# Attention's two ends in a two-layer transformer kernel: the order of the query scale, the number of leading weight units, and the place of the last weight casts

## The chip, the cores and the metric

The kernel runs on one core of a Trainium2 chip. The metric is the device time of one execution in microseconds; before the change the median of three runs is 1749.79 us (1749.52 to 1751.82). The core has five engines that run side by side, each through its own queue in order: TensorE (PE, matrix products into PSUM), VectorE (DVE), ScalarE (ACT), GpSimd (POOL) and SyncE (SP, which here only issues DMAs). PEld in the profile is TensorE's loading of the stationary operand, which overlaps its products.

## The reference

Two layers work on 256 tokens of width 2048. The first is a Fourier mixer; the second, which the change touches, is attention over a window with 256 further context keys, and a final norm:

```python
q, k, v, z = split(h @ w_in)                  # 64 query heads, 8 key/value heads, 64 wide
q = axial_rope(q, rows, cols); k = axial_rope(k, rows, cols)
s = q @ concat(k_window, k_context).T * 64 ** -0.5
p = softmax(concat(s + mask, sink))[..., :-1]
y = (p @ concat(v_window, v_context)) * silu(z)
x = x + gate * (y @ w_out[1])
out = rmsnorm(x, final_g)
```

All inputs are float32. By their shapes, query weights, gate weights and output weights of the attention layer are 33.5 MB each; the page counts 419 MB read from memory in all.

## The kernel before, in words

Products are made to nearly float32 precision from two parts of each operand: a high part (a cast, on ScalarE) and a low part (what is left, a subtraction, on VectorE or GpSimd). `mm3` (lines 144 to 147) then issues three matmuls: high by high, high by low, low by high. A weight load of 1 MB (`raw`, line 47, three buffers, SP's queue) is split in halves by `half_split` (which records lines 66 and 67) or, for half-precision parts with a power-of-two scale, by `split16` (lines 137 and 138). The parts lie in a pool of six buffers (`ws`), so parts of three halves fit when each half needs two.

The order on each engine is not the program's order. A planner sorts the instructions of each engine when the program is built, by program order as priority, by its own estimate of when operands and buffers are ready, and by edges written by hand: `with tc.issue_after(x)` makes the instructions of the block that run on x's engine come behind x.

The attention stage has three sorts of work.

*Filler units* (`units`, `emit_unit`) are the weight products, 142 of them in a fixed order: eight units for each of eight query head groups ("q"), two for each of 32 gate blocks ("z"), and 14 for the first quarter of the output projection ("o"). A q or an o unit is 12 matmuls over 512 columns, a z unit 24 over 256. When a unit is emitted, the weights of the next one are prepared (`prep`). Emission of the last unit of a q group calls `finish_q`; that of the second z unit ends a gate block.

*Query finishing.* `finish_q` takes the two halves (128 tokens each) of a head group's queries from PSUM: ScalarE squares them for a sum (line 1365), VectorE turns them by the rotary step (`roped`, lines 1129 to 1138: one product with the cosines, two with the sines, one sum), and four short VectorE instructions (lines 1371 to 1374) make a power-of-two scale `up` and its counterpart `sc`. `q_parts` (lines 1382 and 1383) makes the scaled high and low parts of each half and turns them: by DMA for seven head groups, and for head group 0 by TensorE (`pe_turn`, line 1392, eight transposes of 128 by 128 and a copy from PSUM, line 1393, on ScalarE for the first half and on VectorE for the second). The calls of `q_parts` are kept in `defer` and made some units later.

*Blocks.* 32 blocks of two heads each. `stage_s(b)` makes the scores (12 matmuls, line 1500), the mask and maximum (VectorE, line 1503), the exponentials (ScalarE, line 1507), the normed parts of the probabilities (ScalarE, line 1522, and VectorE, line 1523), and turns them: by DMA for blocks 0 to 30, and for block 31 by `pe_turn`, called from the block loop. `stage_o(b)` multiplies the turned probabilities with the values (24 matmuls, line 1534).

The order around the change is this: `first` = 10 units, then the query parts of head group 0 and their transposes, and then for b = 0 to 32: `stage_s(b)`, four filler units, `stage_o(b - 1)`. In the last round (b = 32) there are no scores; three units run, then the 32 transposes for block 31, `stage_o(31)`, and one unit. TensorE is held to this order by `issue_after(pe_last[0])`, where `pe_last` is the last matmul so far; the transposes of `pe_turn` do not set it.

Behind it comes the output projection's next half (`wo1b`): 16 groups of 1 MB, each split (lines 137 and 138) and multiplied in 24 matmuls. The splits of every group are held behind `f_last`, the last parts of block 31's probabilities. `first_rest` puts the last two units of the first quarter between groups 1 and 2.

Of the kernel before, what the change touches and what calls it, by code (L numbers as in the profile page):

```python
# [17 lines left out]
P = 128  # L18
# [14 lines left out]
def tile_dit(ctx: ExitStack, tc: tile.TileContext, a: dict, out: bass.AP):  # L33
    nc = tc.nc
    V, S, PE, GP = nc.vector, nc.scalar, nc.tensor, nc.gpsimd
# [4 lines left out]
    actp = ctx.enter_context(tc.tile_pool(name="act", bufs=33))  # L40
# [14 lines left out]
    def act(dt=F32):  # L55
        return actp.tile([P, 512], dt, tag="act", name="act")
# [582 lines left out]
    for g in range(G):  # L639
        for j in {13: (8, 9), 14: (10, 11)}.get(g, (g - 5,) if 5 <= g < 13 else ()):  # L640
            t = up.tile([P, 1024], F32, name="pz", tag="pz", bufs=1)
# [217 lines left out]
    with tc.tile_pool(name="yp", reuse_waits="tile", bufs=32) as ypool:  # L859
# [39 lines left out]
        if True:  # L899
# [44 lines left out]
            for b in range(4, NB):  # L944
# [9 lines left out]
                o = psum()  # L954
# [76 lines left out]
        for i in range(32):  # L1031
            sw, kg = i // 16, i % 16
            if kg == 0:
                o = [psum() for _ in range(8)]
# [23 lines left out]
            if kg >= 12:  # L1058
                for k in range(sw * 8 + (kg - 12) * 2, sw * 8 + (kg - 12) * 2 + 2):
                    t = act()  # L1060
# [43 lines left out]
    with tc.issue_after(st_end[0]):  # L1104
        o = psum()
# [23 lines left out]
    def roped(dst, src, tb, pool, tag="rt", eng=V, tab=rope):  # L1129
        t2 = pool.tile([P, 512], F32, tag=tag, name="rt")  # L1130
        sv = src.rearrange("p (h d) -> p h d", d=64)
        eng.tensor_tensor(dst.rearrange("p (h d) -> p h d", d=64), sv, tab[:, 0, tb, :].unsqueeze(1).broadcast_to([P, 8, 64]), op=ALU.mult)
        s4 = src.rearrange("p (h a t i) -> p h a t i", a=2, t=2, i=16)
        t4 = t2.rearrange("p (h a t i) -> p h a t i", a=2, t=2, i=16)
        sn = tab[:, 1, tb, :].rearrange("p (a t i) -> p a t i", a=2, t=2)
        for t in range(2):
            eng.tensor_tensor(t4[:, :, :, t, :], s4[:, :, :, 1 - t, :], sn[:, :, t, :].unsqueeze(1).broadcast_to([P, 8, 2, 16]), op=ALU.mult)
        eng.tensor_tensor(dst, dst, t2, op=ALU.add)

    with tc.tile_pool(name="h1", reuse_waits="tile", bufs=16) as h1p:  # L1140
# [5 lines left out]
        ident16 = h1p.tile([P, P], F16, name="ident16", bufs=1)  # L1146
        S.copy(ident16, ident)
        kT = []
        with tc.tile_pool(name="kvp", reuse_waits="tile", bufs=2) as kvp:
# [4 lines left out]
            for k in range(KT):  # L1154
                z2 = kvp.tile([P, 1024], F16, tag="hz", name="hz", bufs=16)
                t = kvp.tile([P, 512], F32, tag="ht", name="ht")
# [42 lines left out]
            o = [[psum() for _ in range(2)] for _ in range(4)]  # L1199
# [26 lines left out]
            for tb in range(4):  # L1226
                t, ab = act(), act(F32R)
# [3 lines left out]
                t = act()  # L1231
# [39 lines left out]
        with tc.tile_pool(name="at", reuse_waits="tile", bufs=2) as at:  # L1271
# [55 lines left out]
            def o1_step(k, os_, wh, wl):  # L1327
# [2 lines left out]
                for tb in range(2):  # L1330
                    r = mm3(os_[tb], yh[k][:, tb * P : (tb + 1) * P], yh[k][:, N + tb * P : N + (tb + 1) * P], wh, wl, k == 0, k == NB - 1)
                return r
            slot = [0]

            def k_turn(hp):
                o = psum()
# [12 lines left out]
            def prep_kk(hk):  # L1349
                kkh = at.tile([P, 512], F16, tag="kkh", name="kkh")  # L1350
                kkl = at.tile([P, 512], F16, tag="kkl", name="kkl")
                b = (hk % 2) * 64
                src = kT[hk // 2][b : b + 64, :]
                for c in (0, 64):
                    S.copy(kkh[c : c + 64, :], src)
                for c in (0, 64):
                    GP.tensor_tensor(kkl[c : c + 64, :], src, kkh[b : b + 64, :], op=ALU.subtract)
                kk[hk] = (kkh, kkl)

            def finish_q(hk, oq):  # L1360
                sq = at.tile([P, 2, 4], F32, tag="sq", name="sq")
                qr = []
                for tb in range(2):
                    t = act()
                    S.activation(act(), oq[tb], AF.Square, accum_out=sq[:, tb, 0:1])
                    roped(t, oq[tb], tb, actp, "act")
                    qr.append(t)
                if hk:
                    prep_kk(hk)
                x, up, sc = (sq[:, :, c] for c in (1, 2, 3))  # L1370
                V.tensor_scalar(x, sq[:, :, 0], 2.0**-70, None, op0=ALU.max)
                V.tensor_scalar(x.bitcast(I32), x.bitcast(I32), 24, 23, op0=ALU.logical_shift_right, op1=ALU.logical_shift_left)
                V.tensor_scalar(up.bitcast(I32), x.bitcast(I32), -1.0, 204.0 * 2**23, op0=ALU.mult, op1=ALU.add)
                V.tensor_scalar(sc.bitcast(I32), x.bitcast(I32), kx.bitcast(I32), -30.0 * 2**23 - 2.0**31, op0=ALU.add, op1=ALU.add)
                qt = at.tile([P, 8, 2, P], F16, tag="qt", name="qt")
                qq[hk] = qt, sc
                for tb in range(2):
                    defer.append((slot[0], lambda tb=tb: q_parts(hk, tb, qt, qr[tb], up[:, tb : tb + 1])))
# [10 lines left out]
            def pe_turn(ft, f, tb):  # L1389
                o = pp.tile([P, 8, P], F16, tag="ps", name="ps")  # L1390
                for j in range(8):
                    PE.transpose(o[:, j, :], f[:, j * P : (j + 1) * P], ident16)
                (S.copy if tb == 0 else V.tensor_copy)(ft[:, :, tb, :], o)

            def units():
                order = [("q", 0)]
# [138 lines left out]
                obs[blk, 1] = oo  # L1535
                emit_y(blk)

            first = 10
            for i in range(first):
                emit_unit()  # L1540
                if i == 2:
# [8 lines left out]
            def filler(n):  # L1550
                for _ in range(n):
                    j = slot[0]
                    slot[0] += 1
                    with tc.issue_after(pe_last[0]):
                        emit_unit()
                    if defer and defer[0][0] + 2 < j:
                        defer.pop(0)[1]()

            pts = {}
            for b in range(33):  # L1560
                if b % 4 == 0:
                    while defer:
                        defer.pop(0)[1]()
                y_sums(12, 2 * b if b < 30 else 99)
                if b == 31:
                    out_scale()
                if b < 32:
                    with tc.issue_after(pe_last[0]):
                        pts[b] = stage_s(b)
                filler(4 if b < 32 else 3)  # L1570
                if b:
                    ft, fs = pts.pop(b - 1)
                    with tc.issue_after(pe_last[0]):
                        for (hh, tb), f in fs.items():
                            pe_turn(ft[hh], f, tb)
                        stage_o(b - 1, ft)
                if b == 32:
                    filler(1)


        with tc.tile_pool(name="fin", reuse_waits="tile", bufs=1) as fp:
# [42 lines left out]
            for kg in range(16):  # L1624
                if kg == 2:
                    first_rest()
                t = raw(a["wo1b"][kg])
                with tc.issue_after(f_last[0]), tc.issue_after(f_last[1]):
                    w = [split16(t, i, uw) if kg < 12 else w_scaled(t, i) for i in range(2)]
                if kg + 3 < 12:  # L1630
                    with tc.issue_after(last_cast[0]), tc.issue_after(last_sub[0]):
                        y_half(kg + 3)
                if kg in (3, 5, 7):
                    x2_load(kg // 2)
                for j in range(2):
                    k = kg * 2 + j
                    wh, wl = w[j]
                    for tb in range(2):
                        for c in range(2):
                            q = slice(c * 512, (c + 1) * 512)  # L1640
                            mm3(o[tb][c], *(t[:, tb * P : (tb + 1) * P] for t in y_parts(k)), wh[:, q], wl[:, q], k == 0, k == NB - 1)
# [183 lines left out]
```

## Time and profile before

| what | value |
|---|---|
| median of three runs | 1749.79 us |
| the profiled execution's own time | 1751.69 us |
| its span, first to last instruction | 1749.9 us |
| mean granted TensorE clock | 0.995 |
| busy: TensorE, VectorE, ScalarE, GpSimd | 1708.5, 1376.4, 1103.4, 281.2 us |
| blocks and filler units (first scores to last output) | 1124 to 1610 us |

In a row of a timeline stand the start, the duration, the engine, the line, the operation, what it writes and reads, how many instructions are merged in the row, and in brackets how long the engine sat idle before it and what ended that. Instructions are pipelined, so the time from one start to the next is shorter than a duration. In a row of waits stand the waiting instruction, what it waited for, the total, the number of times and the longest. "adab" is a buffer that is used again for small scales; "raw<-in_wo1b" is a weight load.

### The profile page before, as it was taken

What the parts mean: (1) busy time and instruction counts of PE and PEld (TensorE: products, weight loads), DVE (VectorE), ACT (ScalarE), POOL (GpSimd) and SP (SyncE); (2) the same over time, 40 slices, a digit from 0 to 9 for tenths busy, and PEclk for the clock granted to TensorE, in tenths of its full rate; (3) what the DMA queues carried; (4) which work ended last, traced back from release to release, by engine and by line L of the source; (5) the groups of instructions that cost most, each with busy time, mean ns of one, the idle gap of its engine ahead of it and who ended that gap; (6) DMA issues with size and microseconds to landing.
All of it is one profiled execution on the core that took longest, in us unless ns stands there. A gap on an engine that the chain in (4) does not pass through costs nothing. (4 is left out here: it accounts for less than half of the span.)

```text
span 1749.9 us, 28309 instructions
## 1 busy us (share of the span) xinstructions
PE 1708.5 (98%) x10379; PEld 1131.3 (65%) x10379; DVE 1376.4 (79%) x2390; ACT 1103.4 (63%) x2111; POOL 281.2 (16%) x429
## 2 busy tenths in 40 slices
PE   6999999999999999999999999999999999998997
PEld 4679999644444444446444745688788888975464
DVE  5779888798776787778689585888899888985755
ACT  5545555477777755455335497677777778775643
POOL 0002111211222104202310210200000000050001
PEclk9999999999999999999999999999999999999999
DMA  9998998878998969976997595489999999986643
GB/s 394 417 357 254 275 269 258 304 267 310 342 306 307 314 238 349 388 269 228 393 358 247 147 370 187 138 238 220 235 230 233 218 246 221 233 217 238 236 169 120
DMA packets 249195, 469.94 MB, mean 269 GB/s; under 512 B 171392, under 2 KB 171792, under 8 KB 222176
## 3 DMA queue, kind: packets, MB, share of 16 engines
q1 hardware_dynamic: 197568, 335.60, 59.0%
q0 software_dynamic: 47344, 125.58, 22.6%
q10 hardware_dynamic: 4144, 6.95, 1.2%
q8 instruction: 81, 1.33, 0.3%
q14 instruction: 58, 0.48, 0.1%
HBM read 419.30 MB, written 12.59 MB: 247 GB/s over the span
## 5 line engine op out<-in xcount | busy, mean ns | idle before, releaser
L67 DVE TENSOR_TENSOR wl<-raw,wh 128x1024 fp32r<-128x1024 f32 x152 | 189.7, 1262 | 50.1 <-ACT wh L66 41.9
L146 PE MATMUL ps<-act,wf 128*128 128x512 f16 x512 | 194.0, 379 | 0.0
L147 PE MATMUL ps<-act,wf 128*128 128x512 f16 x512 | 191.1, 379 | 0.0
L145 PE MATMUL ps<-act,wf 128*128 128x512 f16 x512 | 189.8, 379 | 1.1 <-ACT act L877 0.4
L66 ACT CAST wh<-raw 128x1024 fp32r<-128x1024 f32 x152 | 156.9, 1045 | 46.9 <-PE ps L146 29.9
L145 PE MATMUL ps<-y,wf 128*128 128x512 f16 x448 | 169.8, 379 | 0.8 <-ACT wf L137 0.8
L146 PE MATMUL ps<-y,wf 128*128 128x512 f16 x448 | 169.8, 379 | 0.0
L145 PEld LDWEIGHTS <-wf 128*128 128x128 f16 x960 | 93.8, 98 | 114.0 <-ACT wf L137 4.7
L147 PEld LDWEIGHTS <-wf 128*128 128x128 f16 x960 | 93.9, 98 | 113.1
L147 PE MATMUL ps<-y,wf 128*128 128x512 f16 x448 | 164.9, 379 | 0.0
L146 PEld LDWEIGHTS <-wf 128*128 128x128 f16 x960 | 93.9, 98 | 109.0
L137 ACT ACTIVATE wf<-raw,nrm 128x1024 f16<-128x1024 f32 x56 | 63.5, 1145 | 132.6 <-PE ps L147 73.7
L145 PE MATMUL ps<-h,wh 128*128 128x256 f32 x512 | 144.3, 282 | 0.0
L147 PE MATMUL ps<-h,wl 128*128 128x256 f32 x512 | 142.6, 279 | 0.1
L146 PE MATMUL ps<-h,wh 128*128 128x256 f32 x512 | 142.7, 279 | 0.0
L1507 ACT ACTIVATE p<-ps,mx 128x512 f32<-128x512 f32 x128 | 87.8, 686 | 86.4 <-DVE mx L1503 86.1
L138 DVE SCALAR_TENSOR_TENSOR wf<-raw,tn,wf 128x1024 f16<-128x1024 f32 x64 | 79.8, 1281 | 42.6 <-ACT wf L137 42.6
L829 ACT ACTIVATE act<-act 128x512 f32<-128x512 f32 x178 | 109.4, 616 | 5.2 <-DMA act<-in_wo 4.6
L146 PE MATMUL ps<-wl,h 128*128 128x512 f32 x256 | 101.6, 397 | 0.0
L147 PE MATMUL ps<-wh,h 128*128 128x512 f32 x256 | 101.2, 395 | 0.0
L145 PEld LDWEIGHTS ps<-h,wh 128*128 128x128 f32 x512 | 96.1, 188 | 7.1 <-issue 5.9
L145 PE MATMUL ps<-wh,h 128*128 128x512 f32 x256 | 100.4, 403 | 0.0
(430 smaller groups left out, 4656.4 us busy)
## 6 DMA issues: line engine op xcount, KB each, us to landing
raw<-in_wz SPq DMA_DIRECT2D x64, 1024.0 KB, 5.5
raw<-in_awp SPq DMA_DIRECT2D x32, 1024.0 KB, 12.8
zr<-in_adw SPq DMA_DIRECT2D x64, 512.0 KB, 6.9
wa<-in_adw POOLq DMA_DIRECT2D x64, 512.0 KB, 6.7
act<-in_wo POOLq DMA_DIRECT2D x128, 256.0 KB, 7.4
raw<-in_wo SPq DMA_DIRECT2D x32, 1024.0 KB, 8.4
raw<-in_wq SPq DMA_DIRECT2D x32, 1024.0 KB, 5.3
raw<-in_wu SPq DMA_DIRECT2D x32, 1016.0 KB, 7.2
```

Of the source, the lines that this page charges most:

```text
L66: last_cast[0] = S.copy(h, src).ins
L67: last_sub[0] = eng.tensor_tensor(l, src, h.bitcast(F32), op=ALU.subtract).ins
L137: last_cast[0] = S.activation(w[:, 0], src, AF.Copy, scale=up).ins
L138: last_sub[0] = V.scalar_tensor_tensor(w[:, 1], src, up, w[:, 0], op0=ALU.mult, op1=ALU.subtract).ins
L145: PE.matmul(o, wh, xh, start=start, stop=False)
L146: PE.matmul(o, wh, xl, start=False, stop=False)
L147: return PE.matmul(o, wl, xh, start=False, stop=stop).ins
L829: S.activation(t, t, AF.Square, accum_out=c)
L1507: S.activation(pt[hh, tb], so[hh, tb], AF.Exp, bias=mx[:, hh, tb : tb + 1], scale=-1.0, accum_out=sm[:, hh, tb : tb + 1])
```

## The change: what it does

1. In `finish_q`, both squares come first, then the rotary step of the first half, then three of the four scale instructions, then the rotary step of the second half, then the fourth scale instruction, and last the preparation of the next keys (`prep_kk`), which stood ahead of the scale.
2. `first` is 11: eleven filler units run ahead of the first scores. Each later round has as many units as before, so it has the units one place further on.
3. In the last round one unit runs, then the transposes of block 31's probabilities, one unit, `stage_o(31)`, and one unit. `pe_turn` now sets `pe_last`, so that what is issued "after `pe_last`" comes behind the transposes.
4. `pe_turn` returns its copy. The last copy on ScalarE and the last on VectorE are kept in `turned`. The splits of groups 1 to 15 of the output projection are held behind these two; group 0 is still held behind `f_last`.

```diff
             def finish_q(hk, oq):
                 sq = at.tile([P, 2, 4], F32, tag="sq", name="sq")
-                qr = []
                 for tb in range(2):
-                    t = act()
                     S.activation(act(), oq[tb], AF.Square, accum_out=sq[:, tb, 0:1])
-                    roped(t, oq[tb], tb, actp, "act")
-                    qr.append(t)
-                if hk:
-                    prep_kk(hk)
                 x, up, sc = (sq[:, :, c] for c in (1, 2, 3))
+                qr = [act(), act()]
+                roped(qr[0], oq[0], 0, actp, "act")
                 V.tensor_scalar(x, sq[:, :, 0], 2.0**-70, None, op0=ALU.max)
                 V.tensor_scalar(x.bitcast(I32), ...)
                 V.tensor_scalar(up.bitcast(I32), ...)
+                roped(qr[1], oq[1], 1, actp, "act")
                 V.tensor_scalar(sc.bitcast(I32), ...)
+                if hk:
+                    prep_kk(hk)
...
                 for j in range(8):
-                    PE.transpose(o[:, j, :], f[:, j * P : (j + 1) * P], ident16)
-                (S.copy if tb == 0 else V.tensor_copy)(ft[:, :, tb, :], o)
+                    pe_last[0] = PE.transpose(o[:, j, :], f[:, j * P : (j + 1) * P], ident16).ins
+                return (S.copy if tb == 0 else V.tensor_copy)(ft[:, :, tb, :], o).ins
...
-            first = 10
+            first = 11
...
-                filler(4 if b < 32 else 3)
+                filler(4 if b < 32 else 1)
                 if b:
                     ft, fs = pts.pop(b - 1)
+                    if fs:
+                        with tc.issue_after(pe_last[0]):
+                            for (hh, tb), f in fs.items():
+                                turned[tb] = pe_turn(ft[hh], f, tb)
+                        filler(1)
                     with tc.issue_after(pe_last[0]):
-                        for (hh, tb), f in fs.items():
-                            pe_turn(ft[hh], f, tb)
                         stage_o(b - 1, ft)
...
                 t = raw(a["wo1b"][kg])
-                with tc.issue_after(f_last[0]), tc.issue_after(f_last[1]):
+                with tc.issue_after((turned if kg else f_last)[0]), tc.issue_after((turned if kg else f_last)[1]):
                     w = [split16(t, i, uw) if kg < 12 else w_scaled(t, i) for i in range(2)]
```

More of the change, by code (lines that the diff above doesn't have):

```diff
@@ L1332, in o1_step @@
                 return r
-            slot = [0]
+            slot, turned = [0], [None, None]
             def k_turn(hp):
```

## The prediction

> **What bounds the kernel now.** I read the page's head first, then TensorE's waits over the whole run, then a table of windows, and last the timeline around the two places that these name. The head:
>
> ```profile
> span 1749.9 us, 28309 instructions
> ...
> PE 1708.5 (98%) x10379; PEld 1131.3 (65%) x10379; DVE 1376.4 (79%) x2390; ACT 1103.4 (63%) x2111; POOL 281.2 (16%) x429
> ```
>
> TensorE is busy for all but 41 us of 1750, so what can be won is idle time and time at a lower clock. Who made TensorE wait, in the whole run (total, times, longest):
>
> ```profile
> PE ps L1534 <- ACT ft L1393: 6.9, 1, 6.9
> PE ps L1392 <- ACT fq L1382: 3.4, 1, 3.4
> PE ps L146 <- DVE wl L67: 1.8, 2, 0.9
> ```
>
> Apart from the start of the kernel, the two long waits are at the two ends of attention: L1392 transposes the first head group's queries, and L1534 multiplies the last block's probabilities. The windows (PE, PEld, DVE, ACT, POOL busy, granted clock, DMA share, GB/s) show what lies between:
>
> ```profile
> 1118.00:1129.00 11.00, 6.87 (x35) 3.81 (x35) 8.16 (x17) 6.85 (x12) 0.00 (x0) 0.69 0.26 97
> ...
> 1200.00:1300.00 100.00, 100.00 (x783) 84.42 (x782) 89.23 (x166) 76.97 (x155) 6.26 (x4) 1.00 0.95 230
> ...
> 1594.00:1602.00 8.00, 1.10 (x15) 0.75 (x13) 3.19 (x5) 4.14 (x5) 0.00 (x0) 0.83 0.98 402
> ```
>
> In the middle TensorE is full at full clock, with VectorE at 89% and the DMA engines at 95%. The middle can therefore give nothing, and a reorder there can only lose. All of the gain must come from the ends.
>
> **The front end, before.** TensorE's timeline from the tenth filler unit's last matmul:
>
> ```profile
> 1117.83 0.39 PE L147 MATMUL ps<-wh,h 128*128 128x512 f32 x1
> 1121.66 2.07 PE L1392 MATMUL ps<-ident,fq 128*128 128x128 f16 x16 [3.44 <-ACT fq L1382]
> 1124.41 1.04 PE L1500 MATMUL ps<-kkh,qt 64*128 64x512 f16 x4 [0.68 <-ACT qt L1393]
> ...
> 1127.09 0.80 PE L145 MATMUL ps<-wh,h 128*128 128x512 f32 x1
> ...
> 1130.53 0.40 PE L145 MATMUL ps<-wh,h 128*128 128x512 f32 x1
> ```
>
> A unit is 12 matmuls at 0.233 us, 2.80 us. The tenth ends at 1118.06, the eleventh runs from 1127.09 to 1130.53, 3.44 us. For full-speed prices of the rest I use the other end:
>
> ```profile
> 1569.92 0.61 PE L1500 MATMUL ps<-kkh,qt 64*128 64x512 f16 x4
> ...
> 1571.32 0.50 PE L145 MATMUL ps<-wh,ys 128*128 128x512 f32 x1
> ...
> 1584.15 0.50 PE L145 MATMUL ps<-wh,ys 128*128 128x512 f32 x1
> ...
> 1592.74 1.96 PE L1392 MATMUL ps<-ident,f 128*128 128x128 f16 x32
> 1601.61 0.37 PE L1534 MATMUL ps<-ft,v 128*64 128x256 f16 x1 [6.90 <-ACT ft L1393]
> ...
> 1606.14 0.40 PE L146 MATMUL ps<-wf,yf 128*128 128x512 f16 x1
> ...
> 1608.85 1.50 PE L1534 MATMUL ps<-ft,v 128*64 128x256 f16 x23
> 1610.28 0.50 PE L145 MATMUL ps<-wh,ys 128*128 128x512 f32 x1
> ...
> 1613.19 0.39 PE L147 MATMUL ps<-wf,yf 128*128 128x512 f16 x1
> ```
>
> One block's scores take 1.40 us there (1569.92 to 1571.32), 32 transposes 1.96, so 16 take 0.98. From 1118.06 to 1130.53 are 12.47 us for 0.98 + 1.40 + 2.80 + about 0.2 of switching = 5.4 us of work: **7.1 us are lost**, 4.1 of them idle (3.44 + 0.68) and 3.0 slow clock.
>
> Why it is late, in VectorE's and then ScalarE's timeline:
>
> ```profile
> 1114.68 1.21 DVE L67 TENSOR_TENSOR wl<-raw,wh 128x1024 fp32r<-128x1024 f32 x1
> 1115.82 0.68 DVE L1138 TENSOR_TENSOR act<-act,rt 128x512 f32<-128x512 f32 x1
> ...
> 1117.68 0.15 DVE L1371 TENSOR_SCALAR sq<-sq 128x2 f32<-128x2 f32 x1
> 1117.75 1.21 DVE L67 TENSOR_TENSOR wl<-raw,wh 128x1024 fp32r<-128x1024 f32 x1
> ...
> 1119.56 1.21 DVE L67 TENSOR_TENSOR wl<-raw,wh 128x1024 fp32r<-128x1024 f32 x1
> ...
> 1120.76 0.22 DVE L1374 TENSOR_SCALAR sq<-sq,ksc 128x2 int32<-128x2 int32 x1
> 1121.64 1.42 DVE L1383 SCALAR_TENSOR_TENSOR fq<-act,sq,fq 128x512 f16<-128x512 f32 x2 [0.66 <-ACT fq L1382]
> ...
> 1118.03 1.04 ACT L66 CAST wh<-raw 128x1024 fp32r<-128x1024 f32 x1 [1.75 <-PE ps L146]
> 1120.88 1.33 ACT L1382 ACTIVATE fq<-act,sq 128x512 f16<-128x512 f32 x2 [1.81 <-DVE sq L1373]
> 1123.34 1.01 ACT L1393 COPY qt<-ps 128x1024 f16<-128x1024 f16 x1 [1.13 <-PE ps L1392]
> ```
>
> The query scale (L1371 to L1373) is finished at 1120.85. It starts only after both rotary halves but for one sum, and the planner put a 1.14 us weight subtraction behind each of its first two links.
>
> **Front, the change.** (a) Scale ahead of the second rotary half: no instruction is added or removed, eight groups of VectorE work change places. The first half is summed at 1116.42 (1115.82 + 0.60). The three links then end between 1116.7 (nothing comes between) and 1118.9 (a subtraction and rotary steps between); I take 1117.7, since the second half's ready steps of 0.3 to 0.6 us now stand next in line. (b) ScalarE: the casts L1382 are at best behind the weight cast that waits for TensorE until 1118.03, so 1119.1; two casts of 0.67 end at 1120.4, and the last VectorE part (1.42 for two) ends at about 1121.2. (c) The eleventh unit covers TensorE from 1118.06 to 1120.86; it needs the subtraction of 1114.68, done at 1115.89. (d) Then 0.98 of transposes with some 0.3 waiting; ScalarE's copy of the first half starts about 1121.5, and by 1123.34 to 1124.41 the scores follow 1.07 later, at 1122.6; twelfth unit at 1124.2. Before, that point was 1130.53: **6.3 us** gained. Bounds: all of the loss, 7.1. If the scale comes no earlier than before, the eleventh unit alone covers 2.8 of the 3.4 idle: transposes at 1121.66, scores at 1123.3, unit at 1124.9, 5.6 gained. If further weight casts and subtractions (1.04 and 1.21) get ahead of the query parts as well, 4.
>
> The row puts no price on a wait between 0.9 us (no slower matmul after it) and 3.44 us (clock 0.69). In proportion, a rest of 0.9 us idle would cost 0.9 / 4.1 x 3.0 = 0.7 us, which the lower bound holds; I take none. [...]
>
> **The tail, before.** From 1584.15 to 1613.19 TensorE spends 29.04 us on three units (8.59), 32 transposes (1.96), the last block's output (1.50), the 22 matmuls of the output projection that the timeline has in between (0.22 each, as the last 12 of them take 2.71 from 1606.14 to 1608.85; 4.8) and one unit (2.8): 19.7 with the 0.1 lost at the seams. **9.3 us are lost**: 6.9 idle, the rest the slow clock of ten matmuls up to 1606.14. The cause:
>
> ```profile
> 1589.90 2.19 ACT L137 ACTIVATE wf<-raw,adab 128x1024 f16<-128x1024 f32 x2 [1.84 <-PE ps L146]
> ...
> 1597.86 2.19 ACT L137 ACTIVATE wf<-raw,adab 128x1024 f16<-128x1024 f32 x2 [5.16 <-DMA raw<-in_wo1b]
> ...
> 1600.57 1.90 ACT L1393 COPY ft<-ps 128x1024 f16<-128x1024 f16 x2
> ...
> 1581.59 2.73 DVE L1523 SCALAR_TENSOR_TENSOR f<-p,sm,f 128x512 f16<-128x512 f32 x4
> ...
> 1586.23 1.22 DVE L67 TENSOR_TENSOR wl<-raw,wh 128x1024 fp32r<-128x1024 f32 x1
> ...
> 1580.44 1.23 DVE L67 TENSOR_TENSOR wl<-raw,wh 128x1024 fp32r<-128x1024 f32 x1 [0.28 <-ACT wh L66]
> ...
> 1579.90 7.90 SPq L50 DMA_DIRECT2D raw<-in_wo1b x2
> ```
>
> The copies of the turned probabilities stand behind a weight cast (second group of the projection) whose load lands at 1597.8. The transposes were over at 1594.7. VectorE's probabilities had been ready at 1584.3.
>
> **Tail, the change.** (a) The casts from the second group on must follow the last turned copies on ScalarE and VectorE, so this stall can't recur. What is queued behind the copies now is those casts and their halvings; TensorE needs them only after the last output, one unit and the first group (24 matmuls, 5.2). (b) The transposes move two units forward: in the old clock the previous output ends at 1584.15, one unit to 1587.0, transposes to 1588.9. The probabilities (1584.3) are 2.7 us early. (c) The next unit (2.8, to 1591.8) covers the copies: two of 0.95 on ScalarE from about 1587.5, or, behind one cast of the first group, to 1591.1; two on VectorE. The last output starts at 1591.8 without waiting. (d) One unit fewer is left for the tail, because it went to the front: its work is moved, not saved, and its weights are converted one unit sooner. So the subtraction of 1586.23, whose end (1587.45) lets the second group's load start, takes the place of the one before it and ends at 1581.7; with the old 10.3 us (1587.5 to 1597.8) the load lands at 1592, its cast ends at 1595.5, and TensorE wants it at 1601. I count **9.0 us**. Bounds: 6.7, if both first-group casts (2.19) and another get ahead of the copies; 11, if the two 0.9 us waits of the third row of waits go as well. For the seven later head groups two things move. The key preparation (two casts, two subtractions on GpSimd a group) goes behind the scale, within a slack of a block or more. The two query transposes, DMAs on SP's queue with the weight loads behind them, go out up to a unit earlier against the scores. That queue stood for them already:
>
> ```profile
> SPq L1385 <- DVE fq L1383: 39.0, 7, 6.6
> ```
>
> TensorE lost nothing by these seven waits, so I cost both at nothing; the cover is the loads already landed, and the collision on VectorE is a rival below. The eleventh unit's own loads and casts fall where the DMA share was 0.26 (1118 to 1129). Behind the tail the projection is TensorE's, so the gain stays to the end.
>
> **Sum.** 6.3 + 9.0 = 15.3 us. The profiled execution took 1751.69, 1.8 beyond its span of 1749.9, and would take 1736.4; it stands 1.9 above the median of the runs, 1749.79, so the median comes to **1734.5 us**. With the bounds, 10.7 to 18: 1732 to 1739. A measurement of this kernel can tell about 0.2%, 3.5 us, from no change.
>
> **Rivals.** *Tail only*: the planner, working again from its own costs, fills the scale's links with subtractions and lets casts that wait for TensorE stand ahead of the query casts, and the idleness returns behind the eleventh unit. For it: it did so before. Against: 2.8 us of cover whatever it does. 1749.8 - 9 = 1741. *Front only*: the first group's casts, which are not held, wait for their load or a buffer ahead of the copies. Against: before, they waited for TensorE, not for DMA. 1749.8 - 6.3 = 1743.5. *No effect*: both queues keep their holes, shifted; 1749.8. *Slower*: each of the seven later query finishes (rotary 2 x 1.86, by 1115.82 to 1117.68, parts 1.42, scale 0.3: 5.4 us of VectorE) now falls one unit nearer to a block's scores, and VectorE at 89% falls behind. It decides once a weight subtraction is later than the one unit of lead, 2.8: then up to 7 x 2.6 = 18.2 is lost against 15.3, 1752.7 or, with the smaller gain, about 1755. Against: not one wait of TensorE is shown in that middle.
>
> **How the numbers follow.** Forecast 0.66, tail only 0.10, front only 0.10, no effect 0.07, slower 0.07. The range from 1731 to 1744 holds the first three, less their edges. Faster by over 0.2%: 0.86; within: 0.07; slower: 0.07.
>
> **What would show it.** Right: at L1392's 16 transposes a wait under 1 us, at L1534 none, clock 1.00 at both ends, the ft copies ahead of the second group's cast, and still no wait in 1200 to 1300. Wrong: a wait of 3 us at the scores, a late copy behind the first group's cast, or new weight waits of TensorE at each query finish.

## The result, and the profile after

The changed kernel takes **1736.47 us** (median of four runs, 1736.23 to 1739.45) against 1749.65 (four runs, 1749.22 to 1751.82): a ratio of 0.9926, 95% interval 0.9909 to 0.9943. The gain is 13.2 us by the medians. The profiled execution took 1736.42, its span is 1734.6, 15.3 below that of before.

The page's head of the changed kernel:

```profile
span 1734.6 us, 28325 instructions
...
PE 1703.1 (98%) x10379; PEld 1129.7 (65%) x10379; DVE 1373.2 (79%) x2390; ACT 1103.8 (64%) x2111; POOL 276.0 (16%) x429
```

TensorE's waits in the changed kernel (total, times, longest), the rows of attention and its fillers. Transposes are now L1391, the copies of turned data L1392, the query casts L1381 and L1382, the scores L1499, the output L1533:

```profile
PE ps L146 <- DVE wl L67: 1.5, 2, 1.1
...
PE ps L145 <- ACT wh L66: 0.5, 1, 0.5
PE ps L1499 <- ACT qt L1392: 0.4, 1, 0.4
PE ps L1391 <- DVE fq L1382: 0.4, 2, 0.3
```

Both long waits are gone. The 3.4 at the transposes is 0.4, the 6.9 at the output is nothing. The windows (PE, PEld, DVE, ACT, POOL, clock, DMA share, GB/s) show both ends full or nearly so and at full clock, and the middle as it was:

```profile
1118.00:1129.00 11.00, 10.06 (x59) 6.85 (x58) 9.23 (x20) 9.69 (x19) 0.00 (x0) 1.00 0.55 191
1200.00:1300.00 100.00, 100.00 (x769) 83.82 (x769) 89.67 (x167) 78.92 (x156) 4.67 (x4) 1.00 0.95 228
1594.00:1602.00 8.00, 8.00 (x38) 4.37 (x37) 5.94 (x10) 6.00 (x9) 0.00 (x0) 1.00 0.68 237
```

**The front.** TensorE's timeline of the changed kernel, from the eleventh unit on, and then ScalarE's and VectorE's:

```profile
1117.30 0.63 PE L145 MATMUL ps<-wh,h 128*128 128x512 f32 x2
...
1120.10 0.67 PE L1391 MATMUL ps<-ident,fq 128*128 128x128 f16 x8
1120.92 0.40 PE L1391 MATMUL ps<-ident,fq 128*128 128x128 f16 x4 [0.15 <-DVE fq L1382]
1121.59 0.40 PE L1391 MATMUL ps<-ident,fq 128*128 128x128 f16 x4 [0.27 <-DVE fq L1382]
1122.42 0.60 PE L1499 MATMUL ps<-kkh,qt 64*128 64x512 f16 x4 [0.44 <-ACT qt L1392]
...
1124.07 0.50 PE L145 MATMUL ps<-wh,h 128*128 128x512 f32 x1
...
1118.98 1.34 ACT L1381 ACTIVATE fq<-act,sq 128x512 f16<-128x512 f32 x2 [0.67 <-DVE sq L1369]
1120.22 1.03 ACT L66 CAST wh<-raw 128x1024 fp32r<-128x1024 f32 x1
1121.36 1.01 ACT L1392 COPY qt<-ps 128x1024 f16<-128x1024 f16 x1
...
1117.05 1.21 DVE L67 TENSOR_TENSOR wl<-raw,wh 128x1024 fp32r<-128x1024 f32 x1
1118.79 0.15 DVE L1369 TENSOR_SCALAR sq<-sq 128x2 int32<-128x2 int32 x1
1118.99 1.21 DVE L67 TENSOR_TENSOR wl<-raw,wh 128x1024 fp32r<-128x1024 f32 x1
```

The tenth unit ends at 1117.30, 0.76 earlier than before. That lies ahead of anything that the change does: a row of matmuls 125 us sooner (L997) already starts 0.77 earlier. The query casts begin at 1118.98, **inside** the eleventh unit, so the first eight transposes follow it at once. The twelfth unit starts at 1124.07; before, eleven units, the transposes and the scores were done at 1130.53. That is 6.46, of which 0.76 was there already: **5.70 us** from the front, 6.77 from the tenth unit's end to the twelfth unit in place of 12.47. Single executions differ here. The kernel of the first experiment below has the same order of instructions and takes 7.40: one subtraction on VectorE ahead of the rotary step took 2.17 us there and 1.21 here. So the front gives 5.1 to 5.7 us, by execution.

**The tail.** ScalarE and TensorE of the changed kernel:

```profile
1583.62 2.19 ACT L137 ACTIVATE wf<-raw,adab 128x1024 f16<-128x1024 f32 x2 [2.35 <-PE ps L146]
1586.34 1.90 ACT L1392 COPY ft<-ps 128x1024 f16<-128x1024 f16 x2
1591.61 2.19 ACT L137 ACTIVATE wf<-raw,adab 128x1024 f16<-128x1024 f32 x2 [3.38 <-DMA raw<-in_wo1b]
...
1583.66 1.96 PE L1391 MATMUL ps<-ident,f 128*128 128x128 f16 x32
1585.43 0.48 PE L145 MATMUL ps<-wh,ys 128*128 128x512 f32 x1
1588.41 0.30 PE L1533 MATMUL ps<-ft,v 128*64 128x256 f16 x1
```

The copies of the turned probabilities now stand ahead of the second group's cast, which waits 3.38 us for its load. They end at 1588.24, under the unit that runs from 1585.43, and the output starts at 1588.41: just in time. The second unit behind the last scores before is the first one behind them now; its third matmul starts at 1574.69 before and at 1567.89 after, 6.80 ahead. From there to the first evacuation of the projection's sums (1623.95 and 1608.60: 15.35 ahead) the change gains **8.55 us**. Between the two ends it gains 0.34 (6.80 less 6.46).

### The profile page after: what moved, and what is told of

Read it like the earlier page. It is cut to its first block, busy times and chain, and to the rows that moved or that the text cites. A ratio compares the mean times of both kernels' runs of the same rounds, so it can differ in the third digit from the quotient of the medians.

```text
span 1734.6 us, 28325 instructions
## 1 busy us (share of the span) xinstructions
PE 1703.1 (98%) x10379; PEld 1129.7 (65%) x10379; DVE 1373.2 (79%) x2390; ACT 1103.8 (64%) x2111; POOL 276.0 (16%) x429
```

## The experiments

Each kernel is the changed one or the one before with one edit. A time is the median of its own runs, beside the median of the kernel before on the same chip and the ratio with its 95% interval. "The control" is the first kernel below, whose instruction order is the changed kernel's. Where a stretch "from the tenth unit's end to the twelfth unit" is compared, the twelfth unit's start is counted back from the thirteenth at full speed (2.80 us), so that matmuls at a slower clock in the twelfth count as lost. By this count the kernel before takes 12.47, the changed kernel 6.87 and the control 7.50.

### The hold alone taken away

```
-  with tc.issue_after((turned if kg else f_last)[0]), tc.issue_after((turned if kg else f_last)[1]):
+  with tc.issue_after(f_last[0]), tc.issue_after(f_last[1]):
```

> The changed kernel without its fourth part: the casts of groups 1 to 15 stand behind block 31's probabilities (f_last), not behind the turned copies. The planner gives the same order of instructions on all five queues as for the changed kernel, so this is also a second timing and a second profile of the changed kernel. Theory A (the transposes' earlier place removes the tail's stall, the hold adds nothing): 1736.5 us within 1.5, no wait at the last block's output, copies ahead of the second group's casts. Theory B (the hold removes it): 1742 to 1746, with the wait at the output back. Since the orders are the same, B could only be right if the profile's order of the changed kernel came about by chance at run time.

1736.62 us (1736.25 to 1740.92) against 1751.11: 0.9923 (0.991 to 0.9935). All five queues have the same instructions in the same order. In attention the waits are the same but for some 0.3 us more at the first transposes, from the slower subtraction told above. Beside early transposes the hold does nothing.

### Ten units first instead of eleven

```
-  first = 11
+  first = 10
-  filler(4 if b < 32 else 1)
+  filler(4 if b < 32 else 2)
```

> The changed kernel with ten leading units instead of eleven; the unit goes back to the last round, ahead of the transposes. The front's measured gain was 5.7 us. Theory A (the eleventh unit's cover is most of it): the query casts come no sooner than in the changed kernel, about 1119, so TensorE stands some 2.4 us ahead of the transposes; the point at which the eleventh unit ends is 2.8 us later, 1739.3, if the clock holds through a wait of 2.4 us, and up to 3.0 more, 1742.3, if it drops as it did after 3.44. Theory B (the scale's earlier place is most of it): within 0.5 us of the changed kernel, 1736 to 1737.

1740.89 us against 1751.11: 0.9942 (0.9928 to 0.9955), 4.3 above the control. TensorE's wait at the transposes in this kernel:

```profile
PE ps L1391 <- ACT fq L1381: 2.3, 1, 2.3
```

2.3 us is what the scale's move leaves of the 3.44. The clock fell to half behind this wait, from 1120.6 to 1127.5. The loss lies between the two times that theory A gave, without and with a fall of the clock. The prediction had no measured price for a wait between 0.9 and 3.44 us and took no clock loss for it; over 2.3 us the clock did not hold.

### The scale in its old place

```
+                qr = []
                 for tb in range(2):
+                    t = act()
                     S.activation(act(), oq[tb], AF.Square, accum_out=sq[:, tb, 0:1])
+                    roped(t, oq[tb], tb, actp, "act")
+                    qr.append(t)
+                if hk:
+                    prep_kk(hk)
...
-                qr = [act(), act()]
-                roped(qr[0], oq[0], 0, actp, "act")
...
-                roped(qr[1], oq[1], 1, actp, "act")
...
-                if hk:
-                    prep_kk(hk)
```

> The changed kernel with the old order in the query finishing (both rotary halves, the key preparation, then the scale); eleven units and the new tail stay. In the changed kernel the query casts started 1.1 us sooner against the end of the tenth unit than before. Theory A (cover by the unit): the casts, transposes and scores come 0.5 to 1.7 us later, 1737.0 to 1738.2, with a wait of 0.8 to 1.5 us at the first transposes and no slower clock. Theory B (the scale's place carries the front): 3 us or more lost, 1739.5 and up, and the clock in the front's window well below 1.

1741.10 us (1739.35 to 1743.5) against 1751.11: 0.9947 (0.9934 to 0.9959), **4.5** above the control, where my theory A said 0.5 to 1.7. A fell. ScalarE and TensorE of this kernel (its tenth unit ends at 1117.65, its eleventh at 1120.45):

```profile
1120.42 1.04 ACT L66 CAST wh<-raw 128x1024 fp32r<-128x1024 f32 x1 [1.74 <-PE ps L146]
1121.37 1.33 ACT L1382 ACTIVATE fq<-act,sq 128x512 f16<-128x512 f32 x2
...
1122.15 0.40 PE L1392 MATMUL ps<-ident,fq 128*128 128x128 f16 x4 [1.53 <-ACT fq L1382]
1122.76 0.40 PE L1392 MATMUL ps<-ident,fq 128*128 128x128 f16 x4 [0.22 <-ACT fq L1382]
1123.44 0.40 PE L1392 MATMUL ps<-ident,fq 128*128 128x128 f16 x4 [0.29 <-DVE fq L1383]
1124.10 0.40 PE L1392 MATMUL ps<-ident,fq 128*128 128x128 f16 x4 [0.27 <-DVE fq L1383]
1124.94 1.04 PE L1500 MATMUL ps<-kkh,qt 64*128 64x512 f16 x4 [0.44 <-ACT qt L1393]
```

A weight cast that needs a buffer read by the **eleventh unit** stands ahead of the query casts on ScalarE and waits for that unit's end. The unit that should cover the query's work thus holds it up. Then the clock falls at 1124.92, in the scores (1.04 us for four matmuls instead of 0.60). Not all of the 4.5 is the front: from the tenth unit's end to the twelfth unit this kernel takes 10.40, 2.9 more than the control. Another 1.7 us went in this execution to a second fall of the clock at 1551.6, which the last section tells of.

### The eleventh unit alone, and the scale alone

Both on the kernel before. First:

```
-  first = 10
+  first = 11
-  filler(4 if b < 32 else 3)
+  filler(4 if b < 32 else 2)
```

> The kernel before with the eleventh unit alone: old scale order, late transposes, no hold. Front by theory A (cover): 4 to 5.2 us gained. The tail's load starts a unit sooner (2.8 us), so its 6.9 us wait shrinks to about 4: 1740.5 to 1743. Theory B (the unit only moves the wait, and the scale's place is needed): under 2 us at the front, 1745 to 1748.

1749.27 us (11 runs) against 1750.35: 0.999 (0.9982 to 0.9999). Neither theory's range was met; theory B's mechanism, a unit that only moves the wait, is what the trace shows. ScalarE's timeline has the same order as in the last kernel, and among TensorE's waits the tail's stays:

```profile
1120.22 1.04 ACT L66 CAST wh<-raw 128x1024 fp32r<-128x1024 f32 x1 [1.75 <-PE ps L146]
1121.17 1.33 ACT L1382 ACTIVATE fq<-act,sq 128x512 f16<-128x512 f32 x2
```

```profile
PE ps L1534 <- ACT ft L1393: 6.2, 1, 6.2
```

From the tenth unit's end to the twelfth unit it takes 10.40 us where the kernel before takes 12.47: 2.07 gained, not the 5.6 that I gave the unit alone. Second, the kernel before with the changed `finish_q` and nothing else (the diff of the scale above, the other way round):

> The kernel before with the new order in the query finishing alone: ten units, late transposes, no hold. The casts come 1.1 us sooner than before, so the wait of 3.44 us at the first transposes becomes about 2.3. Theory A (the clock drop hangs on a wait of about 3.4 us): the clock holds, 3.5 to 4.1 us gained, 1745.6 to 1746.2. Theory B (the clock loss goes with the idle time, or the drop comes anyway): 1.1 to 2 us gained, 1747.7 to 1748.6. A change of the tail by replanning would show at the last block's output, 6.9 us before.

1750.15 us (11 runs) against 1751.13: 0.9996 (0.9987 to 1.0005), by the times no change. In the trace the same stretch takes 11.35: 1.12 gained. Windows of this kernel, of 1 us each:

```profile
1119.00:1120.00 1.00, 0.00 (x0) 0.00 (x0) 1.00 (x4) 0.48 (x1) 0.00 (x0) 1.00 0.44 57
1120.00:1121.00 1.00, 0.69 (x6) 0.43 (x7) 1.00 (x2) 0.86 (x2) 0.00 (x0) 0.50 0.59 156
...
1126.00:1127.00 1.00, 1.00 (x3) 0.82 (x4) 1.00 (x5) 1.00 (x4) 0.00 (x0) 0.59 0.00 0
```

The clock is halved at 1120.00, within a wait of 2.3 us, and is back at 1126.82. Theory A, which had the clock hold, fell; the trace agrees with B. **Unit alone 2.07, scale alone 1.12, both 5.60** by this count (4.97 in the control): the parts need each other. Each of the two alone has half the clock for 3.4 (the unit) or 6.8 us (the scale) in this stretch, both together none, so part of what joins them is the clock.

### What joins them: the weight casts held

The old place of the scale again (the third kernel), but the weights of the 13th and 14th units may only follow the query parts:

```
+  if qpart and pos[0] in (11, 12):          # qpart: last query cast and last query part
+      with tc.issue_after(qpart[0]), tc.issue_after(qpart[1]):
+          ready[pos[0] + 1] = prep(ulist[pos[0] + 1])
```

> The changed kernel with the query scale back in its old place (behind both rotary halves), but the weight casts and subtractions of the 13th and 14th filler units may only follow the last query cast on ScalarE and the last query part on VectorE. The kernel with the old place and free weights lost 4.5 us against its control, with a weight cast that waited 1.74 us for the eleventh unit ahead of the query casts and a subtraction of 1.2 us in the scale's links. Theory A (weight preparations ahead of the query parts are the whole cost; the place of the scale among the rotary steps is none): the scale's three links follow each other, the query casts begin within the eleventh unit, no wait over 0.6 us at the transposes or the scores, full clock: 1736 to 1738.5. Theory B (the scale's own place behind the second half costs the 4.5): waits of 1.5 us or more at the transposes again, 1740 to 1742.

1737.80 us (1737.49 to 1738.17) against 1751.43: 0.9918 (0.9905 to 0.9932). ScalarE's timeline of this kernel, then two rows of TensorE's:

```profile
1119.38 1.34 ACT L1382 ACTIVATE fq<-act,sq 128x512 f16<-128x512 f32 x2 [3.61 <-DVE sq L1373]
1120.63 1.03 ACT L66 CAST wh<-raw 128x1024 fp32r<-128x1024 f32 x1
...
1120.35 1.04 PE L1394 MATMUL ps<-ident,fq 128*128 128x128 f16 x12
...
1122.62 0.61 PE L1506 MATMUL ps<-kkh,qt 64*128 64x512 f16 x4 [0.61 <-ACT qt L1395]
```

Theory A was right in the main: with that cast behind them the query casts begin at 1119.38, inside the eleventh unit, twelve transposes follow the unit without a wait, and the clock holds at the front. From the tenth unit's end to the twelfth unit it takes 6.88, as the changed kernel does. (This execution, too, has a fall of the clock late in the stage, at 1548.1; the 1.7 us that this costs are more than the 1.3 that separate it from the changed kernel.) So the scale's place among the rotary steps is not itself the cause. In the changed kernel the scale is ready 1.15 us sooner and the planner puts the query casts ahead of the waiting cast; that the one is the reason for the other is argued from the two orders. The hold also takes one of two weight subtractions out of the scale's links (the other stays, which theory A did not have) and the one behind them, so the 3.3 us against the third kernel are for all of these together.

The same hold on the changed kernel:

> The changed kernel with the same hold on the weights of the 13th and 14th units. In the changed kernel one subtraction of 1.21 us stands between the scale and the query parts on VectorE, and the transposes still lose 0.15 + 0.27 to the parts and the scores 0.44 to the copy. Theory A (that is what is left at the front): the 0.42 at the transposes go, 0.4 to 1 us less: 1735.5 to 1736.5, not to be told from the changed kernel by times of five runs, but in the trace. Theory B (the held weights come too late for the 13th and 14th units): new waits of TensorE for wh or wl of 1 us or more after the scores, 1737.5 or more.

1736.96 us (1736.17 to 1740.38) against 1751.43: 0.9913 (0.99 to 0.9927), not to be told from the changed kernel. The waits at transposes and scores are 0.22 and 0.61, 0.83 in all, where the changed kernel has 0.86: A's gain did not come, the wait went from the parts to the copy. B's new weight waits did not come either.

### The tail: transposes late, with and without the hold; the hold alone

The changed kernel with the transposes directly ahead of the output again, as before the change, and the hold kept:

```
-  filler(4 if b < 32 else 1)
+  filler(4 if b < 32 else 2)
   ...
                                  turned[tb] = pe_turn(ft[hh], f, tb)
-                        filler(1)
```

> The changed kernel with the last block's transposes directly ahead of its output, as before the change, but with the hold kept: two units, transposes, output, one unit. Theory A (the order of the queue was the cause; the transposes' earlier place only adds cover for the copies): TensorE waits 0.5 to 2 us at the output for two ScalarE copies (1.9 us), clock 1.00, 1737 to 1738.5. Theory B (the copies need the cover of a unit to be ahead of the weight casts' load): a wait of 4 to 7 us with the slow clock behind it, 1741 to 1745.

1737.58 us against 1751.11: 0.9926 (0.9914 to 0.9939), 1.0 above the control and not to be told from it. The tail did not lose that: from the last scores to the first evacuation it takes 41.3 us, the control 41.6. In the middle of this execution, the median one, the clock fell for 3.4 us at 1547.6, which costs 1.7. The same kernel without the hold:

```
-  with tc.issue_after((turned if kg else f_last)[0]), tc.issue_after((turned if kg else f_last)[1]):
+  with tc.issue_after(f_last[0]), tc.issue_after(f_last[1]):
```

> The changed kernel with late transposes and without the hold: eleven units and the new scale order are all that is left of the change. Here the planner does put the second group's casts ahead of the turned copies on ScalarE. The load of that group was done at about 1591.4 in the changed kernel, the transposes would end at 1588. Theory A (a copy behind a cast that waits for a load is the whole of the tail's stall): copies at about 1594, TensorE idle for 4 to 6 us at the output, slow clock behind it, 1741 to 1745. Theory B (with the load a unit sooner the queue's order no longer matters): at most 2 us, 1737 to 1738.5.

1745.22 us (1745.17 to 1746.71) against 1750.35: 0.997 (0.9958 to 0.9982). TensorE's waits at the output, of the kernel with the hold and then of the one without:

```profile
PE ps L1533 <- DVE ft L1392: 0.3, 1, 0.3
```

```profile
PE ps L1533 <- ACT ft L1392: 6.4, 1, 6.4
```

With late transposes the hold is worth 7.6 us by the times and 9.3 in the traces of the tail (50.6 against 41.3); the fall of the clock in the kernel with the hold is the difference. And the hold alone on the kernel before (`pe_turn` returns its copy, `turned` keeps it, nothing else moves):

```
-  pe_turn(ft[hh], f, tb)
+  turned[tb] = pe_turn(ft[hh], f, tb)
-  with tc.issue_after(f_last[0]), tc.issue_after(f_last[1]):
+  with tc.issue_after((turned if kg else f_last)[0]), tc.issue_after((turned if kg else f_last)[1]):
```

> The kernel before with the hold alone: casts of groups 1 to 15 behind the turned copies; ten units, old scale order, late transposes. Theory A (queue order is the cause): the copies start about 1593.8 behind the first group's work, TensorE waits 0.5 to 2 us in place of 6.9 and the clock stays, so 7 to 8.5 us are gained: 1741.2 to 1742.7. Theory B (the held casts come late and hand the wait on to the second group): a new wait of 2 us or more at the projection's first matmuls, 1744 or more.

1741.90 us (1741.11 to 1747.13) against 1750.35: 0.9953 (0.994 to 0.9965), 8.5 gained, as theory A had it, with a wait of 0.3 us at the output. ScalarE of this kernel: the copies ahead of the cast that waits for its load, the other way round than before.

```profile
1591.55 1.93 ACT L1393 COPY ft<-ps 128x1024 f16<-128x1024 f16 x2 [0.69 <-PE ps L1392]
1595.65 2.19 ACT L137 ACTIVATE wf<-raw,adab 128x1024 f16<-128x1024 f32 x2 [2.17 <-DMA raw<-in_wo1b]
```

So the tail's cause is shown in both directions: the copies' place behind a cast that waits for DMA. Either the hold or the early transposes removes it. Having both shows no gain over either.

### One more unit between the first transposes and the first scores

```
             while defer:
                 defer.pop(0)[1]()
+            with tc.issue_after(pe_last[0]):
+                emit_unit()
...
-                if b == 32:
-                    filler(1)
```

> The changed kernel with one more unit between the first head group's transposes and the first scores (the tail's last unit, behind the last output, is gone). It covers the wait for the turned queries' copies, 0.44 and some 0.3 us: 0.5 to 1 us less than the changed kernel if the tail stays without a wait, 1735.5 to 1736. If the tail needs that unit (the first group's weights not ready behind the last output), 1737 to 1739.

1737.33 us (1733.92 to 1738.54) against 1750.35: 0.992 (0.9907 to 0.9933). By the times it can't be told from the changed kernel. In its trace the 0.44 at the copy is gone, and so are the waits of 1.6 us at the first unit of the output projection (0.47 and 1.14 at about 1545 in the changed kernel); one of 1.07 stands at 1583. Its span, 1733.1, is the shortest of all; no kernel here is surely faster than the changed one.

### The kernel before again

No edit: the kernel before, timed and profiled once more.

> The kernel before, unchanged, for a second profile of it. Its profiled execution was 1.9 us above the median of the runs, and the changed kernel's was at its median; the spans differ by 15.3 us, the medians by 13.2. If that profile was an odd execution, this one has a span of about 1747.9 us, and the places where the two profiles differ are outside the two ends; if the profiled executions stand apart as such, it is near 1749.9 again.

1750.08 us (1749.12 to 1755.26) against 1751.13: 0.9993 (0.9983 to 1.0003). The profiled execution has a span of 1753.5 where the first had 1749.9; the expectation fell. What made it longer is told in the last section.

## Why the prediction was right, and where it was not

**The ends and the middle.** It said 6.3 + 9.0 = 15.3 with nothing from the middle. The same points give 5.70 + 8.55 = 14.25, and 0.34 in the middle; the other 0.76 of the 15.3 in the spans lies ahead of the change and is chance. In the control's execution the front gave 0.63 less. That the sum was met to the tenth is thus partly luck.

**Front, (a) and (b).** The third link was to end at 1117.7, at most 1118.9. It ended at 1118.94, which is 1119.70 on the clock of before (+0.76): outside the bound. The planner still puts a 1.21 us subtraction between the second and the third link. The casts were to begin at 1119.1 and began at 1119.74 on that clock. **(c)** held. **(d)** Scores at 1122.6, in fact 1123.18; twelfth unit at 1124.2, in fact 1124.83. The front's term was 0.6 too large, all of it from (a).

**Front, the bounds: wrong.** "If the scale comes no earlier than before, the eleventh unit alone covers 2.8 of the 3.4 idle ... 5.6 gained" measured 2.07, and the bound of 4 for weight casts that get ahead lies above that too. I priced such a cast by its own 1.04 us. It stands there waiting for the end of the very unit that was to be the cover, and so costs a unit. I had the row for it, the cast of 1118.03 with its 1.75 us of waiting for TensorE, and read it as a fixed time instead of one that moves with the units. "2.8 us of cover whatever it does", said against the rival *tail only*, was wrong for the same reason: both kernels with only one part of the front came to that rival's 1741 (1740.89 and 1741.10), by its mechanism in the one with the old scale.

**Front, the clock: wrong.** I took no clock loss for what was left of the wait. The rows that the prediction shows have no wait between 0.9 and 3.44 us, so no run stood behind that. The two kernels with a 2.3 us wait had half the clock for 6.8 us, and the two with the eleventh unit and the old scale, whose longest single wait is 1.5 us, for 3.4 us. It did not count in the sum, since the changed kernel waits 0.86 in three pieces.

**Tail.** The cause, the cast that waits for its load ahead of the copies, and its removal: shown. (a) The hold does what it says but is not what acts in the changed kernel. (b) and (c) held, with 0.17 us to spare. (d) The subtraction that frees the second group's load is not one unit sooner. It stays behind the low parts of the probabilities and of the projection's other operand (L1522, L1313) on VectorE and ends at 1581.17. On the old clock of this place (the output of block 30 ends at 1584.15 before, at 1580.14 after) that is 1585.2, where I had 1581.7. The load lands at 1591.5 instead of 1588, and nobody is late, for TensorE comes to that group at 1598.27. The term was 9.0 and measured 8.55: mis-sized by 0.45. The two waits of 0.9 us, which the upper bound of 11 had go, did not go: 0.47, 1.14 and 0.14 stand in their place.

**Slower, by the query finishes.** No wait of TensorE from the first scores to 1544, 100.00 of 100 us busy from 1200 to 1300 with VectorE at 89.67: nothing of it came. Its time with the smaller gain was added up wrongly: 1749.8 + 18.2 - 10.7 is 1757.3, not 1755.

**The median.** 1734.5 said, 1736.47 measured. The gain was taken off the median, though it was read from an execution that stood 1.9 above its median; that of the changed kernel stood at its own. The profiled execution's 1736.4 was met (1736.42), the median missed by 2.0.

## What to carry to other kernels

Cover that reads from the same buffers as the work behind it can delay the work it should hide: before adding a filler, look which instruction stands ahead of the wanted one on its engine and whether that one waits for the filler's end. Two edits that are each worth little alone (1.1 and 2.1 us) can be worth 5.6 together, so a part that shows nothing by itself is not yet a part to drop. Take a gain read from one execution off that execution's time, and look how far it stands from its median, before saying a median. Before a difference of 1 or 2 us is put down to an edit, look in the trace whether it lies where the edit is: the 1.0 us of the late transposes did not.

## What the runs showed of the hardware that was not expected

**How long the clock stayed low.** Windows of 1 us of the kernel before, at the two ends of attention (the clock is the third number from the right):

```profile
1121.00:1122.00 1.00, 0.34 (x4) 0.34 (x4) 0.36 (x1) 1.00 (x2) 0.00 (x0) 0.74 0.97 410
...
1128.00:1129.00 1.00, 1.00 (x5) 0.78 (x5) 0.99 (x4) 1.00 (x5) 0.00 (x0) 0.85 0.00 0
...
1599.00:1600.00 1.00, 0.00 (x0) 0.00 (x0) 0.96 (x1) 1.00 (x3) 0.00 (x0) 0.67 0.95 393
...
1606.00:1607.00 1.00, 1.00 (x5) 0.41 (x4) 0.00 (x0) 0.00 (x0) 0.00 (x0) 0.91 0.74 311
```

Windows that lie whole in a slow stretch show 0.50, those around it 1.00, so a mean of 0.74 puts the fall at 1121.48, and so on: slow from 1121.48 to 1128.30 and from 1599.34 to 1606.18, 6.82 and 6.84 us. The stretches with half the clock behind the waits told of in the other kernels are 3.4 or 6.8 us long too.

The length of one wait does not say when the clock falls or for how long. The hold alone has the wait of the kernel before at the front, 3.44 us. Its row, and two of its windows:

```profile
1121.05 0.40 PE L1392 MATMUL ps<-ident,fq 128*128 128x128 f16 x4 [3.44 <-ACT fq L1382]
```

```profile
1121.00:1122.00 1.00, 0.73 (x10) 0.57 (x11) 0.97 (x2) 0.61 (x1) 0.00 (x0) 0.98 1.04 442
...
1125.00:1126.00 1.00, 1.00 (x9) 0.31 (x4) 0.94 (x3) 0.02 (x1) 0.00 (x0) 0.81 0.00 0
```

Its clock fell at 1121.96, behind the wait, and was back at 1125.38, 3.42 us later. In the kernel before it fell at 1121.48, within the wait (1118.22 to 1121.66), and was low for 6.82. The scale alone fell at 1120.00, 2.0 us into a wait of 2.3 (1118.00 to 1120.30), and was low for 6.82. What sets when it falls and for how long is not shown by these rows. At the lower clock transposes took longer as well: in the kernel before 32 took 1.96 us at full clock and 16 took 2.07 at half.

Whether the 0.86 us of waiting that is left at the front of the changed kernel can bring a fall is open: its profile and those of the control, the late transposes and the held weights show no fall there.

**The same wait, with and without a fall.** Eight of the nine kernels with eleven leading units wait 1.6 to 2.1 us at the first unit of the output projection, at about 1545 to 1551. In four of the profiled executions the clock fell there for 3.4 us; at half speed (0.50) that is 1.7 us of work: the old scale, the eleventh unit alone, the held weights, and the late transposes with the hold. In the other four (changed kernel, control, late transposes without the hold, changed kernel with held weights) it did not. TensorE and a window of the late transposes with the hold:

```profile
1546.94 0.50 PE L146 MATMUL ps<-wl,ys 128*128 128x512 f32 x1 [1.11 <-DVE wl L67]
...
1547.00:1548.00 1.00, 1.00 (x4) 0.80 (x5) 1.00 (x2) 1.00 (x3) 1.00 (x2) 0.82 0.00 0
```

The control has the same two waits (0.49 and 1.11 against 0.45 and 1.11) and keeps the clock. So a difference of up to 1.7 us between two kernels here can be whether the clock fell at this place, and nothing that the edit does.

**Where executions of one kernel differ.** Two of the fourteen profiled executions were long for their kernel: the second one of the kernel before (span 1753.5 where the first had 1749.9), and that of the changed kernel with held weights (1740.38 where its median is 1736.96). TensorE's waits and two windows of the latter:

```profile
PE ps L997 <- DVE act L991: 1.9, 1, 1.9
```

```profile
996.00:997.00 1.00, 1.00 (x5) 0.76 (x5) 0.34 (x2) 0.00 (x0) 0.00 (x0) 0.64 0.00 0
...
1003.00:1004.00 1.00, 1.00 (x11) 1.00 (x10) 0.00 (x1) 0.69 (x3) 1.00 (x3) 0.95 0.80 270
```

Both have a wait of 1.7 to 1.9 us at L997, the row sums 120 us ahead of attention, and half the clock for 6.8 us behind it; the other twelve wait 0.2 there and keep the clock. It has nothing to do with the change. VectorE, which the row sums wait for, had itself waited for a small load, in the second kernel and (1.39 us) in the first:

```profile
987.53 0.20 DVE L1126 TENSOR_SCALAR nsink<-sink 128x64 f32<-128x64 f32 x1 [1.62 <-DMA sink<-in_sink]
```

That load (32 KB, issued between 980.7 and 981.8 in all fourteen) took 6.6 and 6.4 us from issue to landing in these two and 4.1 to 4.9 in the other twelve, where VectorE does not wait for it. Why it lands later is open. Such executions may be the single high runs of most kernels here (1739.45 of the changed one, 1740.92 of the control), but there is no profile of those, so that is argued, not shown.
